# A decoder step whose planner's table of durations is corrected to what its trace shows

## The chip, the cores and the metric

The kernel runs on one core of one Trainium2 chip. TensorE (PE in the rows, with PEld for its weight loads) multiplies, VectorE (DVE), ScalarE (ACT) and GpSimd (POOL) compute, and SyncE (SP) issues most transfers. The metric is the device time of one execution in microseconds, and the time of a kernel is the median of its runs.

## The reference

One step of a hybrid decoder layer in float32, for a prompt of 1024 tokens and for 8 samples of one token each with 1024 cached tokens in pages. Cut to what matters:

```python
h = rms_norm(x, norm_g) * (1.0 + scale[:, None]) + shift[:, None]      # scale, shift, gate = c @ w_ada + b_ada
proj = h @ w_in                     # q, keys and values, gates of attention, z_a, u, v, z_b, g_a, g_b
...
def nsa_core(...):                  # 8 heads of 64, 2 groups of keys
    p_c = softmax(q kc) * mc        # compressed keys: one for each 32 tokens
    imp = p_c.sum(heads), by blocks of 64 keys
    _, idx = lax.top_k(imp, 8)      # the 8 blocks that a query sees
    o_s = softmax(q k_sel) v_sel    # selected blocks
    o_w = softmax(q kw) vw          # window of 512
...
s_b = tril(W_s) @ layer_norm(v) + b            # in chunks of 128 tokens, then u * s_b
out = x + gate * ((sig(g_a) * (silu(z_a) * o) @ w_a + sig(g_b) * (silu(z_b) * u * s_b) @ w_b) @ w_out)
```

It also returns the new key and value rows and the updated window buffers.

## The kernel before, in words

Nearly all products are made in float32r from high and low halves: a product `A B` becomes `Ah Bh + Ah Bl + Al Bh`, three matmuls into one bank of PSUM. The names show it: `hh` and `hl` are the halves of h, `c0h`, `c0l`, `c1h`, `c1l` those of a block of weights of 128 columns (`c0` and `c1` alternate).

The stages follow each other: modulation and h (in the profile the first 75 us), the token-major projections (to 250 us), the attention of the samples (to 430 us), the attention of the prompt (to 790 us), the merge and the output projection.

Beside the two attentions run the channel-major projections, "fills" in what follows: jobs (`stream(jobs)`) that multiply 128 columns of weights by h in pieces of 344 tokens, 24 matmuls to a piece, six at a time: `mm<-hh,c0h`, `mm<-hh,c0l`, `mm<-hl,c0h`, and the same again. There are 2016 of these matmuls. What of them isn't done when the attention of the prompt ends is done behind it. They have the last rank.

The order is made by `Plan`, while the program is built. Every operation goes through `Plan.engine`, whose line 217 is the line of all instructions in the profile. The work is written as streams (Python generators), each of which yields when it would have to wait for a tile or a bank. `Plan.go` picks the next step: the first in rank among the streams whose awaited time has been reached by TensorE's planned clock, or else the one that waits least. The awaited times are kept by `Plan.op`, which adds the duration that `Plan.cost` gives for an operation to the time at which its engine and its operands are free. `Plan` computes nothing of the result, and what comes out of it is only the order of the instructions of each engine; the engines then wait for each other by semaphores. A clock at its lower level is planned too (`cold`).

In the attention of the prompt there are 16 tiles, (group of heads, 128 queries). `front` turns the queries (`R`), multiplies them by the compressed keys (`mx<-kc,R`), makes the probabilities `ce` and from them `pg` (on GpSimd), and takes the maxima of the scores: `maxima` writes four (head, key tile) pairs to a bank of `mx` (`mx<-L,R`, with the masks `mx<-tri_bf,ident_bf` and `mx<-far_bf,ident_bf` added by bf16 matmuls), and DVE reduces the bank to `bm` (selected branch) or `wm` (window). `BT` is made from these and turned. `scores` writes `st<-R,L` (two matmuls), ACT and others make the exponentials `pt` and their halves `p`, and `outputs` multiplies them by the values, `pv<-p,vv`. There are two banks of each of the tags `mx`, `st`, `pv` and `mm`.

In the attention of the samples the pages of keys are gathered (`gk`, by GpSimd, four buffers) and turned, four blocks at a time, in two halves for each sample (`mx<-main,gk` x4, `turn4`); the scores (`st<-kh,qpad`, `st<-kl,qpad`) of a half come one step later. `drop("gk")` after the second half lets the next gather be issued. `red` is the sum by which pages are compressed.

Of the kernel before, what the change touches and what calls it, by code (L numbers as in the profile page):

```python
# [9 lines left out]
F32 = mybir.dt.float32  # L10
FR = mybir.dt.float32r
# [17 lines left out]
class Pack:  # L29
    """Constants that depend on the shapes alone, as columns of one [128, n] array."""  # L30
# [62 lines left out]
class Plan:  # L93
    """Estimates when the engines get to what has been emitted, so that independent streams of work can be
    emitted in an order in which the engines wait little. It has no part in what is computed."""
# [4 lines left out]
    def __init__(self):  # L100
        self.free, self.bus, self.slots, self.rings, self.seen = {}, 0.0, {}, {}, {}
        self.columns, self.streams, self.last = {}, [], 0.0
        self.gone, self.since, self.spilled = 0.0, {}, {}

# [7 lines left out]
    def slot_free(self, uid, name, bufs):  # L112
        """When the next tile of a ring can be written."""
        key = uid, name, self.rings.get((uid, name), 0) % bufs
        return max([x[2] + 60.0 for x in self.seen.get(key, ())] + [0.0])

    def leave(self, uid):
        """The memory of a pool goes to those that come later, when the accesses to it are over."""
# [12 lines left out]
    def meet(x, y):  # L131
        """Whether two accesses to a tile, as box() gives them, overlap."""
# [8 lines left out]
    def after(self, ap, writes_only, engine=None):  # L141
        """When the accesses to the elements of ap are over."""
# [22 lines left out]
    def cost(self, engine, name, outs, ins, size, start):  # L165
        if engine == "pe":
            n, m, dt = ins[1].free_size(), ins[0].free_size(), ins[0].dtype
            cost, passes = max(n / 2.4 + 2.5, (26 if dt == BF else 104) * m / 128), 1
            if name == "transpose":
                passes = 2  # L170
            elif dt == F32:
                cost, passes = max(4 * n / 2.4, 208 * m / 128), 4
            tick = int(start // self.TICK)
            self.columns[tick] = self.columns.get(tick, 0.0) + passes * n * ins[0].partition_size() / 128
            return cost * (2 if self.cold(start) else 1)
        if engine == "dve":
            plain = name == "tensor_copy" and outs[0].space == ins[0].space
            return 67 + (0.52 if plain else 1.042) * size
        if engine == "act":
            return (280 if len(ins) > 1 else 70) + 0.834 * size  # L180
# [51 lines left out]
    def add(self, gen, rank, filler=False):  # L232
        """A stream of work. It yields None to go on when its last step is done, 0 to go on at once, a time or an AP
        to go on when that is reached or written, a function to go on when that is true."""
        self.streams.append([rank, gen, 0.0, None, filler])

    def go(self, until=None, slack=-100.0):
        """Runs the streams, a step of the first in rank that would not wait, until there are none (or until())."""
# [21 lines left out]
def nsa_gmlp_step(ctx: ExitStack, tc: tile.TileContext, a: dict):  # L260
# [29 lines left out]
    def free_bank(tag):  # L290
        """Goes on when a bank can be written, as far as other streams let it."""
# [15 lines left out]
    def rows(name, n, m=128):  # L307
        """The n elements of an input on each of m partitions."""
# [38 lines left out]
    def rsqrt(out, x, scale, n, p=128):  # L347
        """out = (x * scale + EPS) ** -0.5"""
# [24 lines left out]
    def weights(todo):  # L373
        """Loads slices (key, source, columns) in order and cuts them into hi and lo, but for those used as they are."""
# [46 lines left out]
    def x_turned(first):  # L421
        """RMS-normalised x, transposed: every other tile."""
# [26 lines left out]
    def x_loads():  # L449
        """The tiles of x behind the weights of the modulation, which all wait for."""  # L450
# [38 lines left out]
    def modulation():  # L489
        """Shift and scale of the samples and the prompt (column 8), and from them h."""  # L490
# [54 lines left out]
    def h_split():  # L545
        """h as its halves, as it comes."""
# [27 lines left out]
    def rope_tab(which):  # L574
        """[cos * g | sin * g'] so that rope(x * g) = x * cos_g + swap(x) * sin_g"""
# [9 lines left out]
    def constants():  # L585
        """What P1 needs beside its weights, each in time."""
# [25 lines left out]
    def fold(i, p, n):  # L612
        """The rows of the hi and lo halves of the samples, added."""
# [12 lines left out]
    def norm_rope(p, m, i, nh, t, final, done, x=None):  # L626
        """rope(rms_norm(p) * g) into the parts of final: (first head, end, out)"""
# [85 lines left out]
    def gate_rows():  # L713
        """The gate rows of the modulation, to DRAM until the end."""
# [137 lines left out]
    class Chunk:  # L852
        """128 columns of a weight as hi and lo [128, k, 128]."""
# [17 lines left out]
    def paced():  # L871
        """Whether the jobs are not ahead of the attention, so that they last as long as it does."""
# [27 lines left out]
    def stream(jobs):  # L900
        """Jobs of (source of weights, body, condition): the weights of the next job load while this one runs."""
# [24 lines left out]
    def gate_tanh(p, n):  # L926
        """tanh(p / 2), so that p * sigmoid(p) = p * (1 + tanh(p / 2)) / 2"""
# [24 lines left out]
    def z_body(br, c):  # L952
        """silu(z) of a branch, times x where that is there, to DRAM until the merge."""
# [13 lines left out]
    def products(br):  # L967
        """What the projection of a branch takes, as its halves."""
# [23 lines left out]
    def gate_job(br, c):  # L992
        """tanh of half the merge gates of 128 channels, to DRAM until the merge."""
# [14 lines left out]
    def merge_job(br, j):  # L1008
        """Two chunks of 128 channels of a branch in model width, times the gate: all of m, or added to it."""
# [44 lines left out]
    def hand_over():  # L1054
        """When the rotary parts are done, their space goes to the weights of the jobs."""
# [967 lines left out]
```

## Time and profile before

| | us |
|---|---|
| median of 3 runs (lowest, highest) | 1042.51 (1041.81, 1042.57) |
| profiled execution: span from the first to the last instruction | 1039.6 |
| TensorE busy in it | 1018.3 (98%) |
| DVE, ACT, GpSimd busy | 657.1, 468.5, 305.5 |

The profile has no other time of the profiled execution than its span; the median of the runs is 2.9 us above it. A matmul's busy time in the rows outlasts the start of the next one, since matmuls are pipelined, so what a matmul costs is read from the distance of the starts. TensorE's granted clock was 1.00 in the mean, which is its upper level (2.4 GHz).

### The profile page before, as it was taken

To read this page: it belongs to the slowest core of one execution; us is meant where nothing else is said; L and a number is where in the kernel's file an instruction comes from. 1 tells how busy PE (TensorE), PEld (TensorE's weight loads), DVE (VectorE), ACT (ScalarE), POOL (GpSimd) and SP (SyncE) were. 2 spreads that over 40 slices of the span, in tenths; PEclk is the share of its full clock that TensorE was granted. 3 is DMA by queue.
4 is the path that set the end of the run, shared out by engine and by line. 5 is a ranking of instruction groups with operands and counts; after the bars stand their busy time and mean duration, and the time that the engine had idled before them with its cause. 6 is when DMAs were issued, how large, how long until landed. Compare 5 with 4: busy or idle time off the path is not lost. (4 is left out here: it accounts for less than half of the span.)

```text
span 1039.6 us, 16376 instructions
## 1 busy us (share of the span) xinstructions
PE 1018.3 (98%) x5747; PEld 878.7 (85%) x5747; DVE 657.1 (63%) x1372; ACT 468.5 (45%) x984; POOL 305.5 (29%) x332
## 2 busy tenths in 40 slices
PE   7999999999999999999999999999999999999998
PEld 2589977879999999987878788778788999998776
DVE  5676786354668766578787868895753147675322
ACT  5763332001332244767766677677666242232000
POOL 0453565454221110013334332433333100251000
PEclk9999999999999999999999999999999999999999
DMA  9735451103875745521212121211111478554321
GB/s 328 263 95 175 135 185 52 61 22 129 277 213 149 256 152 192 151 67 41 79 53 72 35 64 49 68 38 51 50 58 59 126 248 254 187 163 146 120 91 62
DMA packets 106311, 130.33 MB, mean 125 GB/s; under 512 B 27299, under 2 KB 71525, under 8 KB 106230
## 3 DMA queue, kind: packets, MB, share of 16 engines
q1 hardware_dynamic: 101622, 112.52, 33.7%
q0 software_dynamic: 4608, 16.78, 5.2%
q8 instruction: 45, 0.74, 0.3%
q14 instruction: 36, 0.29, 0.1%
HBM read 98.95 MB, written 30.23 MB: 124 GB/s over the span
## 5 line engine op out<-in xcount | busy, mean ns | idle before, releaser
L217 PE MATMUL pv<-p,vv 128*128 128x512 f32 (+1 forms) x396 | 111.7, 399 | 0.5 <-DVE p L217 0.4
L217 PE MATMUL mm<-hh,c0h 128*128 128x344 f32 x320 | 105.3, 329 | 0.0
L217 ACT ACTIVATE pt<-st 128x512 f32<-128x512 f32 x132 | 78.7, 596 | 58.5 <-PE st L217 56.1
L217 PE MATMUL mm<-hh,c1h 128*128 128x344 f32 x320 | 104.9, 328 | 0.0
L217 PE MATMUL mm<-hl,c0h 128*128 128x344 f32 x320 | 102.3, 320 | 0.0
L217 PE MATMUL mm<-hl,c1h 128*128 128x344 f32 x320 | 102.2, 319 | 0.0
L217 PE MATMUL mm<-hh,c1l 128*128 128x344 f32 x320 | 102.2, 319 | 0.0
L217 PE MATMUL mm<-hh,c0l 128*128 128x344 f32 x320 | 102.2, 319 | 0.0
L217 PE MATMUL st<-R,L 128*128 128x512 f32 (+1 forms) x264 | 88.2, 415 | 0.0
L217 PEld LDWEIGHTS pv<-p,vv 128*128 128x128 f32 (+1 forms) x396 | 65.7, 172 | 22.4 <-DVE p L217 1.9
L217 DVE TENSOR_TENSOR p<-pt,p 128x512 fp32r<-128x512 f32 x88 | 69.4, 794 | 17.7 <-ACT p L217 17.1
L217 POOL TENSOR_TENSOR p<-pt,p 128x512 fp32r<-128x512 f32 x44 | 60.0, 1364 | 53.9 <-ACT p L217 53.9
L217 ACT ACTIVATE p<-pt 128x512 fp32r<-128x512 f32 x94 | 59.1, 629 | 13.6 <-POOL pt L217 12.3
L217 POOL TENSOR_SCALAR_AFFINE_SELECT pt<-pt 128x512 f32<-128x512 f32 x40 | 29.3, 732 | 121.7 <-ACT pt L217 119.8
L217 PE MATMUL mx<-L,R 128*128 128x512 f32 (+3 forms) x204 | 61.7, 364 | 1.8 <-DVE bm L217 1.1
L217 PEld LDWEIGHTS mm<-hh,c1h 128*128 128x128 f32 x320 | 60.3, 188 | 2.9 <-issue 0.2
L217 PEld LDWEIGHTS mm<-hh,c0h 128*128 128x128 f32 x320 | 60.4, 189 | 2.5 <-issue 0.2
L217 PEld LDWEIGHTS mm<-hh,c1l 128*128 128x128 f32 x320 | 60.3, 188 | 2.5
L217 PEld LDWEIGHTS mm<-hh,c0l 128*128 128x128 f32 x320 | 60.3, 188 | 2.1
L217 PEld LDWEIGHTS mm<-hl,c0h 128*128 128x128 f32 x320 | 60.1, 188 | 0.0
L217 PEld LDWEIGHTS mm<-hl,c1h 128*128 128x128 f32 x320 | 60.1, 188 | 0.0
L217 ACT ACTIVATE th<-mm 128x344 f32<-128x344 f32 x68 | 30.9, 454 | 58.3 <-PE mm L217 58.0
(497 smaller groups left out, 2669.3 us busy)
## 6 DMA issues: line engine op xcount, KB each, us to landing
t_db<-th SPq DMA_DIRECT2D x24, 172.0 KB
t_da<-th SPq DMA_DIRECT2D x24, 172.0 KB
th<-t_db SPq DMA_DIRECT2D x24, 172.0 KB
th<-t_da SPq DMA_DIRECT2D x24, 172.0 KB
graw<-in_w_ada_dram SPq DMA_DIRECT2D x16, 256.0 KB
araw<-in_w_ada_dram SPq DMA_DIRECT2D x16, 256.0 KB
xt<-in_x_dram SPq DMA_DIRECT2D x8, 512.0 KB
eraw<-in_w_ada_dram SPq DMA_DIRECT2D x16, 256.0 KB
```

Source lines behind the costliest of these rows:

```text
L217: r = getattr(real, name)(*args, **kw)
```

## The change

The durations in `Plan.cost` are replaced, and an attribute is added that holds the form of TensorE's last instruction. Nothing else differs but comments. No operation is added, removed or given to another engine.

```diff
 def __init__(self):
+        self.form = "split"
...
     def cost(self, engine, name, outs, ins, size, start):
         if engine == "pe":
             n, m, dt = ins[1].free_size(), ins[0].free_size(), ins[0].dtype
-            cost, passes = max(n / 2.4 + 2.5, (26 if dt == BF else 104) * m / 128), 1
-            if name == "transpose":
-                passes = 2
-            elif dt == F32:
-                cost, passes = max(4 * n / 2.4, 208 * m / 128), 4
+            form, passes, turn = "split", 1, 0.0
+            if dt == FR and name != "transpose":
+                cost = max(0.4375 * n + 7, 104 * m / 128)
+                turn = {"split": 0.0, "full": 85.0, "part": 190.0}[self.form]
+            elif name == "transpose" or dt == BF:
+                form, passes = "full", 2 if name == "transpose" else 1
+                cost = max(0.4375 * n + 7, (26 if dt == BF else 104) * m / 128)
+                turn = 190.0 if self.form == "part" else 0.0
+            elif m <= 64 and n > 128:
+                form, passes, cost = "part", 4, 0.4375 * n * 4 * m / 128 + 3
+                turn = 0.0 if self.form == "part" else 140.0
+            else:
+                form, passes, cost = "full", 4, max(4 * (0.4375 * n + 7), 208 * m / 128)
+                turn = 190.0 if self.form == "part" else 0.0
+            self.form = form
             tick = int(start // self.TICK)
             self.columns[tick] = self.columns.get(tick, 0.0) + passes * n * ins[0].partition_size() / 128
-            return cost * (2 if self.cold(start) else 1)
+            return cost * (2 if self.cold(start) else 1) + turn
         if engine == "dve":
             plain = name == "tensor_copy" and outs[0].space == ins[0].space
+            if name == "reciprocal":
+                return 80 + 18 * size
             return 67 + (0.52 if plain else 1.042) * size
         if engine == "act":
-            return (280 if len(ins) > 1 else 70) + 0.834 * size
+            moved = ins and self.box(ins[0])[1][0] != self.box(outs[0])[1][0]
+            return (280 if len(ins) > 1 else 70) + 0.834 * size + (105 if moved else 0)
```

Here `n` is the number of columns that a matmul streams, `m` the columns of its weights, `FR` float32r, `BF` bf16 and `F32` plain float32. `moved` is an activation whose output begins on another partition than its input.

The new order differs in most of the two attentions. The first place is TensorE's order in the seventh tile of the prompt's attention, behind the second bank of maxima; `L_4485` and `L_4363` are the same keys, `R` the queries, `far_bf` and `tri_bf` the masks. Before:

```order
L217 MATMUL mx<-L_4485,R 128x384
L217 LDWEIGHTS ident_bf
L217 MATMUL mx<-far_bf,ident_bf 128x128
L217 MATMUL st<-R,L_4484 128x512
L217 MATMUL st<-R_5516,L_4487 128x512
L217 MATMUL mm<-hh,c0h 128x344
L217 MATMUL mm<-hh,c0l 128x344
L217 MATMUL mm<-hl,c0h 128x344
L217 MATMUL mm<-hh,c0h 128x344
L217 MATMUL mm<-hh,c0l 128x344
L217 MATMUL mm<-hl,c0h 128x344
L217 MATMUL mx<-L_4485,R 128x256
```

And after:

```order
L231 MATMUL mx<-L_4363,R 128x384
L231 LDWEIGHTS ident_bf
L231 MATMUL mx<-far_bf,ident_bf 128x128
L231 MATMUL st<-R,L_4362 128x512
L231 MATMUL st<-R_5313,L_4365 128x512
L231 MATMUL mx<-L_4363,R 128x256
L231 LDWEIGHTS ident_bf
L231 MATMUL mx<-tri_bf,ident_bf 128x128
L231 MATMUL mx<-L_4363,R 128x256
L231 LDWEIGHTS ident_bf
L231 MATMUL mx<-far_bf,ident_bf 128x128
L231 MATMUL mx<-L_4363,R 128x384
```

The six fills between the scores and the next maxima are gone from here.

The second place is TensorE's order in the keys of the samples, from one half's turned keys to the next half's; `main` holds the identity, `qpad` the queries of the samples. Before, up to the second of them (ahead of these rows stand the first, its two score matmuls and one more fill):

```order
L217 MATMUL mm<-hh,c0l 128x344
L217 MATMUL mm<-hl,c0h 128x344
L217 MATMUL mm<-hh,c0h 128x344
L217 MATMUL mm<-hh,c0l 128x344
L217 MATMUL mm<-hl,c0h 128x344
L217 MATMUL mm<-hh,c0h 128x344
L217 MATMUL mm<-hh,c0l 128x344
L217 MATMUL mm<-hl,c0h 128x344
L217 MATMUL mm<-hh,c0h 128x344
L217 MATMUL mm<-hh,c0l 128x344
L217 MATMUL mm<-hl,c0h 128x344
L217 MATMUL mx<-main,gk 128x128 x4
```

And after, with both:

```order
L231 MATMUL mx<-main,gk 128x128 x4
L231 MATMUL pv<-pd,red 128x32
L231 MATMUL st<-kh,qpad 128x512
L231 MATMUL st<-kl,qpad 128x512
L231 MATMUL mm<-hh,c1h 128x344
L231 MATMUL mm<-hh,c1l 128x344
L231 MATMUL mm<-hl,c1h 128x344
L231 MATMUL mm<-hh,c1h 128x344
L231 MATMUL mm<-hh,c1l 128x344
L231 MATMUL mm<-hl,c1h 128x344
L231 MATMUL mx<-main,gk 128x128 x4
```

Of the 12 fills between the two halves six are left; in the other half of a sample there are 12 as before.

## Rows read from the trace of the kernel before

**Rows 1.** The page's first line.

```profile
span 1039.6 us, 16376 instructions
```

**Rows 2.** Busy time (instructions) of PE, PEld, DVE, ACT, POOL by stretch; clock, DMA share, GB/s.

```profile
0.00:75.00 75.00, 66.93 (x314) 40.35 (x315) 49.95 (x127) 49.68 (x108) 25.63 (x45) 1.00 0.68 236
75.00:250.00 175.00, 174.40 (x890) 148.61 (x889) 108.61 (x235) 40.99 (x81) 90.09 (x78) 1.00 0.31 99
250.00:430.00 180.00, 177.88 (x1178) 172.18 (x1179) 119.36 (x217) 69.18 (x158) 33.39 (x37) 1.00 0.65 207
430.00:790.00 360.00, 354.44 (x2032) 296.43 (x2031) 267.98 (x599) 249.93 (x537) 121.77 (x137) 1.00 0.19 57
790.00:1035.00 245.00, 244.69 (x1342) 221.11 (x1340) 109.92 (x195) 58.69 (x104) 34.61 (x36) 1.00 0.48 152
```

**Rows 3.** Timeline of PE, keys of the samples: start us, duration us, [idle before <-releaser].

```profile
259.10 0.63 PE L217 MATMUL mx<-main,gk 128*128 128x128 f32 x4 [1.27 <-DVE red L217]
...
268.19 0.60 PE L217 MATMUL mx<-main,gk 128*128 128x128 f32 x4
...
274.00 0.60 PE L217 MATMUL mx<-main,gk 128*128 128x128 f32 x4
...
275.12 0.32 PE L217 MATMUL mm<-hh,c0h 128*128 128x344 f32 x1
...
276.85 0.32 PE L217 MATMUL mm<-hl,c0h 128*128 128x344 f32 x1
277.59 0.63 PE L217 MATMUL mx<-main,gk 128*128 128x128 f32 x4 [0.41 <-DMA gk<-in_cache_k_slc_dram,idx]
```

**Rows 4.** Timeline of PE, the seventh tile of the prompt's attention.

```profile
534.87 0.53 PE L217 MATMUL mx<-kc,R 128*128 128x64 f32 x4
...
536.99 0.23 PE L217 MATMUL mx<-far_bf,ident_bf 128*128 128x128 bf16 x1
...
538.94 0.42 PE L217 MATMUL mx<-L,R 128*128 128x384 f32 x1
...
539.43 0.40 PE L217 MATMUL mm<-hh,c0h 128*128 128x344 f32 x1
539.67 0.32 PE L217 MATMUL mm<-hh,c0l 128*128 128x344 f32 x1
```

**Rows 5.** DVE's groups by form, 430 to 790 us: busy us, mean ns | idle before.

```profile
L217 DVE TENSOR_TENSOR p<-pt,p 128x512 fp32r<-128x512 f32 x84 | 66.6, 798 | 12.7 <-ACT p L217 12.2
L217 DVE TENSOR_REDUCE bm<-mx 128x8 f32<-128x512 f32 x72 | 47.5, 682 | 4.1 <-PE mx L217 3.8
```

**Rows 6.** Timeline of DVE at the place of rows 4.

```profile
536.61 1.34 DVE L217 TENSOR_REDUCE wm<-mx 128x4 f32<-128x512 f32 x2
```

**Rows 7.** Waits of PE, 430 to 790 us: us in total, times, longest.

```profile
PE mx L217 <- DVE bm L217: 1.7, 4, 0.8
PE mx L217 <- DVE BT L217: 1.6, 2, 1.0
PE mx L217 <- DVE s L217: 0.6, 1, 0.6
...
PE mx L217 <- DVE wm L217: 0.2, 1, 0.2
```

**Rows 8.** Timelines of PE and POOL: the chain to `pg` in two tiles.

```profile
540.25 0.41 POOL L217 TENSOR_TENSOR pg<-ce,gates 128x128 f32<-128x128 f32 x1
...
702.81 0.53 PE L217 MATMUL mx<-kc,R 128*128 128x64 f32 x4
...
707.01 0.40 POOL L217 TENSOR_TENSOR pg<-ce,gates 128x128 f32<-128x128 f32 x1 [2.92 <-DVE ce L217]
```

**Rows 9.** The gathers `gk` on POOL, 250 to 300 us.

```profile
DMA to landing us min/median/max: 4.2/5.1/8.4
```

**Rows 10.** Timeline of PE in the modulation.

```profile
16.84 1.02 PE L217 MATMUL mm<-araw,cT 128*9 128x512 f32 x2
```

**Rows 11.** ACT's groups by form, 430 to 790 us.

```profile
L217 ACT ACTIVATE R<-mx 32x128 fp32r<-32x128 f32 x64 | 17.1, 267 | 7.2 <-PE mx L217 6.4
```

## The prediction

> **What bounds the kernel now.** I read the page first, then the stages, then the waits of each stage, then the timeline around the places where the order of TensorE's instructions changes. The span is 1039.6 us [rows 1], and in the five stretches [rows 2] TensorE's busy times add up to 1018.3. They show where the rest lies: length minus busy is 8.1 us in the first 75 us, 0.6 us in the token-major projections, 2.1 us in the decode attention, 5.6 us in the prompt attention, and 0.3 us in the end. The granted clock is 1.00 throughout, so no stretch gains or loses by it. A program of fixed TensorE work that is 98% busy gets faster only by shorter waits (about 17 us of them, 8 in the beginning, which the change hardly reorders), and slower by longer ones. In the attention the other engines are near: DVE works 268 and ACT 250 of 360 us. The fills (2016 matmuls of 344 columns) cover them.
>
> **Is the corrected number right?** Twelve fills in a row start from 275.12 to 276.85, 0.157 us each [rows 3]; the old table says 344/2.4+2.5 = 146 ns, the new one 157.5. Behind a masking matmul of the form "full" the step is 539.43 to 539.67, 0.24 us [rows 4], so 0.08 more: the new turn of 85 ns. DVE's reductions of a maximum (682 ns) and its products of probabilities (798 ns) [rows 5] stand at 67+1.042x512 = 600 ns in both tables. So before, TensorE's fills were planned 7% short and DVE's long operations 12% and more, and the plan was nearly a true picture on a faster clock. Now TensorE alone is right, and what it waits for is still planned short. That is the core of my forecast: a fill is now thought to cover 7% more than before, so fewer are put into a chain, while the chain is as long as it was.
>
> The Trainium skill, TensorE: Matmul & The Clock Gate, section Back-to-back issue gap, gives N/2.4+2.5 ns for an isolated matmul at the upper clock, which is the old table and speaks against the change. The trace does not agree: 157 ns instead of 146. By the rule the fills that I count below as withdrawn would be worth 26 us instead of 28, and the sum would be smaller by half a microsecond.
>
> **The change part by part.** No work is added. TensorE's order has 292 turns from full to split instead of 298; at the 0.08 us above that is **-0.5 us**.
>
> Prompt attention. By the order, 708 fills stand in it instead of 888, and 540 behind it instead of 258 (102 fewer stand ahead of it). 180 x 0.157 = 28 us of cover leave a stage whose waits are 5.6 us. What is late next is the pair of `mx` banks: the maxima write one, DVE reduces it (`bm`, `wm`), and two writes later TensorE needs it again. The first place in the order above is such a one: the bank closed at 536.99 is written again at 538.94, 1.95 us later, with DVE's two reductions over at 536.61+1.34 = 537.95 [rows 4, 6]. Without the six fills the second write comes 0.94 us sooner, at 538.0, so here it just fits. I did this for all 111 places where a write follows a `bm` or `wm` reader, adding the start-to-start times of what stands between. Two queued reductions take 1.3 us [rows 6]; cover under that is had at 7 places before and 27 after, and what is missing adds up to 2.6 and 9.0 us: **+6.4 us**. The check: the trace's waits of matmuls for `bm` and `wm` are 1.7 and 0.2 us in five places [rows 7], and as a matmul's row (0.32 us) outlasts its step (0.16), each such wait is longer than it shows by 0.16, so 2.7 us, against 2.6 counted. Bounds: with an answer of 1.0 us (DVE with a short queue; one reduction and the way there and back) it is 0.9 to 2.2, +1.3; with 1.5 us (a further product ahead in DVE's queue) 4.6 to 15.3, +10.7. I take the middle one because it is the one that meets the trace.
>
> The other chain of a tile goes from the scores of the compressed keys (`mx<-kc,R`) to the gated probabilities (`pg`), which TensorE then turns. It takes 534.87 to 540.66, 5.8 us, in the seventh tile, and 702.81 to 707.41, 4.6 us, in the fourteenth [rows 4, 8]. By the order TensorE's cover is 6.1 us or more in all 16 tiles before; after, it is 3.99 in the fourteenth, 4.73 to 5.73 in six others. With 4.6 us everywhere 0.6 us are missing, with 5.8 us 4.3. I take **+0.6 us**, the value of the tile that is shortest.
>
> Decode. Before, 12 fills stand between the turned keys of one half of a sample and those of the next; after, 6 and 12 in turn (second place above). Each load has four buffers and its gather is issued when an earlier one is dropped. From the second half of one sample to the first of the sample after next is 268.19 to 277.59 us before; without the 0.41 us waited for the gather, and the 0.16 us that the row hides, 8.83 us [rows 3]. After it is 12 fills less, 8.83-12x0.157 = 6.95 us. Gathers land 4.2/5.1/8.4 us after issue [rows 9]: the median stays covered, the slowest is late by 8.4-6.95 = **+1.5 us**. The first keys already wait 1.27 us for `red` [rows 3], and come six fills (0.9 us) sooner, with nothing to bring the gather forward: **+0.9 us**. Bounds for decode: 0 (the slow one was issued early) and +6 (four late ones).
>
> The first 75 us and the token-major projections. The order there is almost the one before. The new table gives `mm<-araw,cT` 66+140 ns, but two of them take 1.02 us [rows 10], so they are still planned short, and I see no place in the order that this moves against a wait. 0, within 1.5 us either way.
>
> ACT's 105 ns and DVE's reciprocals. `R<-mx` over 32 partitions takes 267 ns [rows 11]; the old table said 70+0.834x128 = 177, the new 282. This is the one part that makes the plan of other engines truer, and it acts the right way (more cover ahead of `BT` and `R`). Its effect is already in the order I counted.
>
> Sum: -0.5+6.4+0.6+1.5+0.9 = **+8.9 us**. The profiled execution's span of 1039.6 us becomes 1048.5; the runs' median, 1042.51, lies 2.9 us above it, which I carry over: **1051 us**.
>
> **The rivals.** *Same* (within 0.2%, some 2.1 us, which is what a measurement of this kernel can tell): the withdrawn fills were surplus, as at the first place, where the bank is free at 537.95 and would be asked for at 538.0; and the answer to a lone reduction is 1.0 us. Then -0.5+1.3+0.9 = +1.7, 1044 at most. Against it: DVE's load rises from 74 to some 81% of a stage shorter by 28 us, so that two reductions queue oftener.
> *Faster*: the moved evictions, now planned 105 ns longer each (four `R` in a row, 0.42 us), put cover where TensorE waits for `BT` (1.6 us, two times) and `s` (0.6 us) [rows 7] and for what ACT gives. If these 2.2 us go, the 0.5 us of turns, and about half of the 1.9 us at the banks, it is -3.7, **1039**. It decides in favour of this if DVE answers a bank within 0.95 us, the cover at the first place; the shown queue of two is against it.
> *Decode bound by its gathers*: the period of a sample falls from 5.81 us (268.19 to 274.00) [rows 3] to 4.87 (six fills less); if landings, not TensorE, set the pace then, each of the six later samples loses the 0.94 again, 5.6 us in place of the 1.5: +13 in all, **1055**.
>
> **How the numbers follow.** My forecast, +4 to +12 us, gets 0.54; decode bound, above, 0.12; same, 0.15; faster by over 2.1 us, 0.19. Together slower 0.66, same 0.15, faster 0.19. The likeliest case alone gives 1046 to 1055; eight in ten take in part of the faster case (down to 1039) and the upper bound of the banks with some of decode's (up to 1062).
>
> **What would show it.** Right: the attention shorter by about 20 us, the end longer by some 44 (282 x 0.157), TensorE's waits for `bm` and `wm` two to four times the 1.9 us, in about 20 places; the decode with one or two waits for `gk` above 1 us. Wrong: waits for `bm` and `wm` as now although the fills are gone (DVE had idle time just there), or the waits for `BT` and `s` gone; or a new wait in the first 75 us, where I claim nothing moves.

## The result, and the profile after

The changed kernel takes 1081.58 us (median of 4 runs) against 1042.44 us before: a ratio of 1.038, 95% interval 1.0365 to 1.0395. The direction was forecast, the size was not: +39 us instead of +9, far outside the range.

First the span and the stretches, as in [rows 1] and [rows 2], but with the border at 802 us, where the last output of the prompt's attention starts.

```profile
span 1079.7 us, 16393 instructions
```

```profile
0.00:75.00 75.00, 62.20 (x259) 34.36 (x260) 46.42 (x114) 45.77 (x96) 26.95 (x41) 0.95 0.69 227
75.00:250.00 175.00, 174.21 (x875) 146.82 (x874) 106.83 (x243) 42.49 (x88) 88.26 (x80) 1.00 0.32 100
250.00:430.00 180.00, 173.15 (x1146) 165.79 (x1144) 121.08 (x219) 68.30 (x155) 35.52 (x40) 1.00 0.62 197
430.00:802.00 372.00, 350.94 (x1933) 281.23 (x1933) 267.33 (x601) 253.30 (x544) 126.51 (x142) 1.00 0.18 53
802.00:1075.00 273.00, 273.00 (x1541) 251.96 (x1539) 111.62 (x195) 58.66 (x105) 29.52 (x30) 1.00 0.48 148
```

In the kernel before, that border lies at 805 us and not at the 790 of [rows 2]. Its row there:

```profile
430.00:805.00 375.00, 369.44 (x2112) 309.60 (x2111) 272.31 (x606) 259.54 (x555) 126.71 (x142) 1.00 0.19 58
```

TensorE's idle time grows in three places: 12.8 us in the first 75 (8.1 before), 6.9 in the samples' attention (2.1), 21.1 in the prompt's (5.6). In the first stretch the granted clock, 1.00 before, is 0.95 in the mean.

Idle time misses the part of a wait that a matmul's row hides. So below I count a wait as what the distance of two starts exceeds the usual one of the same shapes, behind and ahead of the same forms, in the kernel before. By this count TensorE's work is 1001.7 us in both traces, and its waits are 27.4 us before and 67.2 after: 39.8 us, the whole difference of the spans (40.1). Steps that are longer because the clock was lower are in it. By stages, the first up to the last turned tile of x, then up to the first turned keys `gk`, to the first `mx<-kc,R`, to the last `pv<-p,vv`, to the end:

| waits, us | first | projections | samples | prompt | end |
|---|---|---|---|---|---|
| before | 8.3 | 3.5 | 2.8 | 12.0 | 1.0 |
| after | 17.6 | 5.0 | 7.7 | 36.7 | 0.2 |

What is called usual is a choice: with the median or the lower quartile of each distance single entries move by up to 4 us, the differences between the two kernels by about 1.

TensorE's waits in the attention of the prompt, 430 to 802 us (total, times, longest), answer to [rows 7]:

```profile
PE mx L231 <- DVE BT L231: 4.3, 5, 1.5
PE mx L231 <- DVE bm L231: 3.2, 5, 0.8
PE mx L231 <- DVE s L231: 2.8, 5, 1.4
PE pv L231 <- POOL p L231: 2.8, 4, 1.2
PE mx L231 <- DVE wm L231: 2.6, 8, 0.5
PE mx L231 <- DVE ce L231: 2.4, 3, 1.4
PE mx L231 <- ACT pgT L231: 1.5, 3, 0.7
```

The banks behind `bm` and `wm`, on which the prediction put nearly all, are 5.8 of these 19.6 us. Five other answers are late too, and longer than before.

The place of [rows 4] and [rows 6] in the kernel after, first TensorE's rows and then DVE's:

```profile
533.51 0.23 PE L231 MATMUL mx<-far_bf,ident_bf 128*128 128x128 bf16 x1
533.54 0.71 PE L231 MATMUL st<-R,L 128*128 128x512 f32 x2
...
534.52 0.44 PE L231 MATMUL mx<-L,R 128*128 128x384 f32 x1
```

```profile
533.13 1.33 DVE L231 TENSOR_REDUCE wm<-mx 128x4 f32<-128x512 f32 x2
```

The reductions end at 534.46 and the bank is written at 534.52: the six fills were surplus here, as computed. It is otherwise where DVE has other work. At a later tile the bank is wanted behind six fills and two score matmuls, and DVE is in the selection and the output of another tile:

```profile
637.73 0.63 PE L231 MATMUL st<-R,L 128*128 128x512 f32 x2
639.20 0.30 PE L231 MATMUL mx<-main,pg 128*128 128x128 f32 x1 [0.84 <-DVE bm L231]
```

```profile
637.42 0.72 DVE L231 TENSOR_SCALAR imp<-imp 128x16 f32<-128x16 f32 x1
638.06 0.19 DVE L231 RECIPROCAL s<-s 128x8 f32<-128x8 f32 x1
638.28 0.17 DVE L231 TENSOR_TENSOR s<-s,g 128x8 f32<-128x8 f32 x1
638.37 1.28 DVE L231 TENSOR_REDUCE bm<-mx 128x8 f32<-128x512 f32 x2
```

The reductions begin only when three operations of other chains are over, at 638.37; the answer is not two reductions but whatever stands ahead of them in DVE's order. (The first of the three takes 0.72 us and not some 0.17; the last section comes back to it.) And a whole chain can be late, here that of `BT`, behind six fills of which the last starts at 502.66. TensorE's row, then two of DVE's ahead of it:

```profile
504.47 0.30 PE L231 MATMUL mx<-main,BT 128*128 128x128 f32 x1 [1.49 <-DVE BT L231]
```

```profile
503.01 0.51 DVE L231 TENSOR_SCALAR BT<-cst 128x4 f32<-128x4 f32 x1
503.62 0.70 DVE L231 TENSOR_SCALAR BT<-cst 128x8 f32<-128x8 f32 x1
```

In the samples' attention the two waits that were forecast are there (TensorE's timeline, then the gathers, as in [rows 3] and [rows 9]):

```profile
267.51 0.63 PE L231 MATMUL mx<-main,gk 128*128 128x128 f32 x4 [2.30 <-DVE red L231]
...
283.82 0.63 PE L231 MATMUL mx<-main,gk 128*128 128x128 f32 x4 [2.00 <-DMA gk<-in_cache_k_slc_dram,idx]
```

```profile
DMA to landing us min/median/max: 4.5/5.9/8.1
```

### The profile page after: what moved, and what is told of

Its sections match the earlier page's. It is cut to its first block, busy times and chain, and to the rows that moved or that the text cites. A ratio compares the mean times of both kernels' runs of the same rounds, so it can differ in the third digit from the quotient of the medians.

```text
span 1079.7 us, 16393 instructions
## 1 busy us (share of the span) xinstructions
PE 1033.5 (96%) x5747; PEld 880.2 (82%) x5747; DVE 654.7 (61%) x1372; ACT 468.5 (43%) x984; POOL 306.8 (28%) x332
## 5 line engine op out<-in xcount | busy, mean ns | idle before, releaser
L231 PE MATMUL mm<-hh,c1h 128*128 128x344 f32 x280 | 91.7, 327 | 0.0
L231 PE MATMUL mm<-hh,c0h 128*128 128x344 f32 x280 | 91.1, 326 | 0.0
L231 PE MATMUL mm<-hh,c0l 128*128 128x344 f32 x280 | 89.5, 320 | 0.6 <-DVE c0l L231 0.6
L231 PE MATMUL mm<-hl,c0h 128*128 128x344 f32 x280 | 89.4, 319 | 0.0
L231 PE MATMUL mm<-hh,c1l 128*128 128x344 f32 x280 | 89.4, 319 | 0.0
L231 PE MATMUL mm<-hl,c1h 128*128 128x344 f32 x280 | 89.4, 319 | 0.0
L231 ACT ACTIVATE p<-pt 128x512 fp32r<-128x512 f32 x94 | 59.1, 629 | 21.2 <-POOL pt L231 16.7
L231 POOL TENSOR_TENSOR m<-m,th 128x344 f32<-128x344 f32 x24 | 25.2, 1070 | 143.1 <-DVE th L231 143.1
L231 PEld LDWEIGHTS mm<-hh,c0l 128*128 128x128 f32 x280 | 52.7, 188 | 3.2 <-DVE c0l L231 0.9
L231 PEld LDWEIGHTS mm<-hh,c0h 128*128 128x128 f32 x280 | 52.7, 188 | 2.9 <-issue 0.4
L231 PEld LDWEIGHTS mm<-hh,c1l 128*128 128x128 f32 x280 | 52.7, 188 | 1.9
```

Of the source, the lines that this page charges most:

```text
L231: r = getattr(real, name)(*args, **kw)
```

## The experiments

The fills are counted here from the first to the last row of the prompt's maxima and outputs, as in the expectations (846 before, 654 after). Theory A is that of the prediction in its general form: TensorE's durations grew and the others' did not, so the plan puts too little cover into the chains. All but e15, e16 and e17 ran once; the kernel before, which ran beside them, lay between 1039.55 and 1042.68 us, so that 3 us between single runs say nothing. "Waits" are those of the table above.

**One half of the change each.** e1 takes back ACT's and DVE's entries, e2 has only them.

```diff
# e1, against the change
-            if name == "reciprocal":
-                return 80 + 18 * size
-            moved = ins and self.box(ins[0])[1][0] != self.box(outs[0])[1][0]
-            return (280 if len(ins) > 1 else 70) + 0.834 * size + (105 if moved else 0)
+            return (280 if len(ins) > 1 else 70) + 0.834 * size
# e2: these lines of the change, in the kernel before
```

> The new durations of TensorE alone; ACT's 105 ns and DVE's reciprocals are taken back. Theory A (TensorE's cover is now planned longer than what it covers, because TensorE's durations grew and those of DVE, ACT and GpSimd stayed about a tenth short): the whole loss is there, 1078 to 1086 us; by the order 606 fills stand in the attention of the prompt (654 with the whole change, 846 before, counted from the first maxima to the last output), so if anything a little slower than 1081.6. Rival B (the lengthened moved activations and reciprocals put the order of the prompt's attention out of step): most of the loss goes, under 1060 us. Rival C (any change of the table costs about as much, since the order before was a lucky one): 1060 to 1100, no relation to the count of fills.

> The table of before with only ACT's 105 ns for moved operands and DVE's reciprocals corrected. Theory A: TensorE's scale is unchanged, 834 fills in the attention (846 before), so 1038 to 1048 us. Rival B: 1060 us or more. Rival C: any, likely 1055 or more, though the count of fills is that of before.

e1: 1090.42 us, waits of the prompt's attention 41.2 us. e2: 1050.74, waits there 19.2. So the loss is TensorE's table (e1 lies above theory A's range, on its side). ACT's and DVE's entries cost 9.6 us alone, though the whole change is 9 us faster with them than without. That e2 should stay under 1048 was wrong.

**The scale.** e3 shortens TensorE's new durations, e4 lengthens the others', e8 lengthens TensorE's old ones.

```diff
# e3, against the change
-            return cost * (2 if self.cold(start) else 1) + turn
+            return 0.93 * (cost * (2 if self.cold(start) else 1) + turn)
# e4, against the change
-            cost = self.cost(engine, name, outs, ins, size, start)
+            cost = self.cost(engine, name, outs, ins, size, start) * (1 if engine == "pe" else 1.1)
# e8, against the kernel before
-            return cost * (2 if self.cold(start) else 1)
+            return 1.07 * cost * (2 if self.cold(start) else 1)
```

> The whole change, with all of TensorE's new durations (turns too) times 0.93, so that the scale of TensorE to the other engines is about that of before, while the corrected proportions among TensorE's own forms stay. Theory A: most of the loss goes; 780 fills in the attention, a third of the way from before to the change, so 1045 to 1060 us. Rival D (it is the proportions: turns and the part form put the first 75 us and the chains wrong): stays above 1070. Rival C: any, likely 1055 or more.

> The whole change, and the durations of DVE, ACT and GpSimd times 1.1, to about what the trace shows. Theory A: the scales fit again and the fills come back into the attention (858 by the order; 846 before), so 1038 to 1055 us. Rival D: stays above 1070. Rival C: 1055 or more.

> The table of before with all of TensorE's durations times 1.07 and nothing else: the scale of the change with the proportions of before. 738 fills in the attention (846 before, 654 with the change). Theory A: a good part of the change's loss, 1052 to 1068 us, by waits in the prompt's attention, the first stage as before. Rival D (turns and forms, not the scale): 1040 to 1047.

e3: 1062.21 us (waits in the prompt's attention 19.6); e4: 1059.04 (15.7); e8: 1056.82 (19.1). Half or more of the loss goes with the scale from either side, and the new scale of TensorE alone makes 15 us (e8). But e3 and e4 lie 2 and 4 us above theory A's ranges, and e4 has 858 fills in the attention, more than the kernel before, with more waits (15.7 instead of 12.0). In e3 and e4 the first stage keeps its loss (16.2 and 14.0 us of waits), so it has another cause.

**The turns.** e10 is the change without them, e11 the kernel before with one of them.

```diff
# e10, against the change
-            return cost * (2 if self.cold(start) else 1) + turn
+            return cost * (2 if self.cold(start) else 1)
# e11, against the kernel before
+            split = dt == FR and name != "transpose"
+            turn, self.form = 85.0 if split and not self.form else 0.0, split
...
-            return cost * (2 if self.cold(start) else 1)
+            return cost * (2 if self.cold(start) else 1) + turn
```

> The whole change with the turns (85, 140 and 190 ns) at nothing. The slopes of the new table stay. 798 fills in the attention (654 with the turns, 846 before). Theory G (the turns, which the old table did not have at all, take more cover than the 7% of the slope): the attention's waits fall to 18 to 24 us, 1060 to 1070 us. Rival (the slope is what counts): 1075 or more.

> The table of before with one thing of the new one: 85 ns when a split matmul follows another form. 732 fills in the attention (846 before; 738 when all of TensorE's durations were planned 1.07 times as long, which gave 1056.8). Theory G: 1054 to 1066 us, waits of the attention 18 to 26 us. Rival: 1042 to 1049.

e10: 1069.86 us; the waits of the prompt's attention are 19.5, and those of the first stage even 22.2. e11: 1062.03, waits of the attention 24.5. So the turn of 85 ns alone adds more waits to that stage (12.5 us) than a slope of 7% does (7.1 in e8). Both leave nearly the same number of fills in it (732 and 738), so the difference isn't one of their count.

**The cover itself.** e9 leaves every duration of the change and asks for a margin.

```diff
# e9, against the change
-    plan.go(until=lambda: 1 in closed)
+    plan.go(until=lambda: 1 in closed, slack=400.0)
```

> The whole change, but in the attention of the prompt a stream counts as ready only when TensorE's planned clock is 400 ns past its awaited time (before and in the change: 100 ns ahead of it). The durations stay those of the change; only the cover grows: 1026 fills in that attention by the order (654 with the change). Theory A (the loss of that stage is lost cover, whatever the table says): the stage's waits fall from 36.7 us to 8 to 16, 1055 to 1064 us; what is left is the first stage and the decode, which the edit leaves alone. Rival F (the new order itself is the trouble, such as which stream comes first at an engine): still above 1072.

e9: 1063.61 us. The waits in the attention fall from 36.7 to 10.5, less than before the change, with 1026 fills there (846 before): with enough cover that stage's loss goes, whatever the durations say. Its rows answer to the first list above:

```profile
PE mx L231 <- DVE BT L231: 2.0, 4, 0.8
PE mx L231 <- DVE wm L231: 1.7, 5, 0.5
PE mx L231 <- DVE bm L231: 0.3, 1, 0.3
```

But 162 fills are left behind it, and the end waits 8.3 us (1.0 before). e12 shows that side more strongly, with too much cover in the kernel before.

```diff
# e12, against the kernel before
-            cost = self.cost(engine, name, outs, ins, size, start)
+            cost = self.cost(engine, name, outs, ins, size, start) * (1 if engine == "pe" else 1.1)
```

> The table of before with the durations of DVE, ACT and GpSimd times 1.1, about as the trace has them; TensorE's stay short. It gives more cover than before: 888 fills in the attention and 144 behind it (258 before), at the banks 0.7 us missing at an answer of 1.3 us (2.6 before). Theory A: the attention's 12 us of waits fall to 6 to 10, so 1035 to 1043 us, unless the first stage gets out of step (then up to 1050). Rival C: 1050 or more.

e12: 1070.72 us, a miss of 28. The end, with 144 fills, waits 17.1 us, and the attention 16.7 (12.0 before), although 888 fills stand in it. In this stretch behind the attention TensorE is busy for 85 of 100 us and its clock falls:

```profile
800.00:900.00 100.00, 85.28 (x456) 76.14 (x455) 38.45 (x75) 43.05 (x88) 18.85 (x23) 0.90 0.45 137
```

The fills are a budget: what is added in the attention is missing in the merge, where 162 fills (e9) and 144 (e12) were too few.

**The first stage.** e5 takes the form `part` out of the change, e6 puts it alone into the kernel before.

```diff
# e5, against the change
-            elif m <= 64 and n > 128:
-                form, passes, cost = "part", 4, 0.4375 * n * 4 * m / 128 + 3
-                turn = 0.0 if self.form == "part" else 140.0
# e6, against the kernel before
+            elif dt == F32 and m <= 64 and n > 128:
+                cost, passes = 0.4375 * n * 4 * m / 128 + 143, 4
```

> The whole change without the form part: the matmuls of the modulation with 9 columns of weights and 512 streamed are again planned at about 0.9 us instead of 0.07 (0.21 with its turn). Behind the first 75 us or so the order on TensorE is that of the change. Theory E (the wrong price of this form is what costs the first stage its 6 to 9 us): 1072 to 1077 us, with waits of the first stage near the 8.3 us of before. Rival (the first stage is lost by the new scale of TensorE, as the attention is): 1080 to 1083.

> The table of before with only this form at its new price (69 ns and a turn of 140). Behind the first stage the order on TensorE is that of before. Theory E: 1047 to 1052 us, the loss all in the first stage. Rival: 1040 to 1044.

e6: 1049.92 us, the waits of the first stage 15.8 instead of 8.3: this price alone costs what the theory said. e5: 1082.63, and 15.5 us there: taking it out gives nothing back in the time, against the theory, and 2.1 us in that stage's waits. In both runs a part is the clock. Here are the first 75 us of e5:

```profile
0.00:75.00 75.00, 63.42 (x272) 38.21 (x273) 47.21 (x114) 46.54 (x99) 23.44 (x41) 0.93 0.69 229
```

The mean clock of that stretch is 0.93 in e5, 0.95 in e6 and in the kernel after, and 1.00 before. The missing shares of 75 us, 5 and 4 us, are an estimate of what the clock can have taken there; over the whole span e5's clock was 0.991 in the mean and that of the kernel after 0.996, which is 5 us more. So e6 shows that the price of this form is enough to put the stage out of step; what it costs inside the whole change e5 doesn't settle. In e5, in e6 and in the kernel after, the last product with the modulation's weights (`araw`) comes late, at 40.13 us in e5, at 40.52 in e6. Here it is in the kernel before, and then in the kernel after:

```profile
36.54 1.02 PE L217 MATMUL mm<-graw,cT 128*9 128x512 f32 x2
37.40 1.02 PE L217 MATMUL mm<-araw,cT 128*9 128x512 f32 x2
```

```profile
41.29 1.02 PE L231 MATMUL mm<-graw,cT 128*9 128x512 f32 x2
42.15 1.02 PE L231 MATMUL mm<-araw,cT 128*9 128x512 f32 x2
```

One of them costs 0.86 us by the starts (36.54 to 37.40; a row with x2 is one product, which the trace has as two records); the old table said 4x512/2.4 = 853 ns, the new one 66 and a turn of 140. Here the correction replaced a true number by a false one.

**One stage each.** e13 has the new table until h is there, e14 in the prompt's attention alone. In both the old formulas stand beside the new ones, and a flag chooses.

```diff
# e13 and e14, in cost(), against the change
+            if not self.new:
+                ...
+                return cost * (2 if self.cold(start) else 1)
# e13 starts with self.new = True
     plan.go(until=lambda: len(h_ready) == NT + 1, slack=100.0)
+    plan.new = False
# e14 starts with self.new = False
     plan.go(until=lambda: "decode" in over and jobs_done[0] >= b_jobs)
+    plan.new = True
```

> The new table for the first stage alone (until h is there), the old one from then on. Behind the first stage the order on TensorE is that of before. If the stages' losses add up (theory H), this is the first stage's 6 to 9 us: 1048 to 1052 us, and waits in the attention of the prompt as before, 11 to 13 us. Rival: the first stage's loss is made good later, 1041 to 1044.

> The new table for the attention of the prompt alone, the old one until then. 678 fills in it (654 with the whole change, 846 before). Theory H: this stage's loss alone, waits of 30 to 38 us there instead of 12: 1060 to 1068 us. Rival: the attention lost because of what it was handed by the stages before it, under 1055.

e13: 1048.67 us (before, in the same runs, 1041.59), waits of the first stage 16.6. e14: 1062.98, waits of the attention 34.5. The two lose 7.1 and 21.4 us, 28.5 of the 39; of the rest 6.4 us are the waits that the projections and the samples' attention gained.

**How much any disturbance costs, and a version that beats both.** e7 makes a step that corrects nothing; e16 gives the kernel before a little more margin; e15 and e17 give the new table its margin in the attention alone, e17 without ACT's and DVE's entries; e18 is one of these entries alone.

```diff
# e7, against the kernel before
-            cost, passes = max(n / 2.4 + 2.5, (26 if dt == BF else 104) * m / 128), 1
+            cost, passes = max(n / 2.4 + 3.0, (26 if dt == BF else 104) * m / 128), 1
# e15 and e17, against e14; e16 (with 0.0), against the kernel before
-    plan.go(until=lambda: 1 in closed)
+    plan.go(until=lambda: 1 in closed, slack=150.0)
# e17 also, as e1; e18, against the kernel before: the two lines on `moved` of the change
```

> The table of before with 3.0 instead of 2.5 ns behind n/2.4: TensorE's durations 0.3% longer, which corrects nothing. It asks how much any disturbance of the order costs. Theory A (scale): 1042 to 1048 us, since 804 fills stand in the attention instead of 846 and the banks are covered better than before (1.2 us missing at an answer of 1.3 us, 2.6 before). Rival C (the order before was a lucky one): 1050 us or more.

> The kernel before, with a margin of 0 instead of 100 ns ahead in the attention of the prompt: 882 fills in it and 222 behind it. It asks whether the kernel before had the right amount of cover. Theory A: 1036 to 1043 us, waits of the attention 7 to 12 us. Rival C: 1046 or more.

> As the one before, and in that stage a stream counts as ready only when TensorE's planned clock is 150 ns past its awaited time, instead of 100 ns ahead of it. 870 fills in the attention and 240 behind it (846 and 258 before). Theory A: with the cover back, and the true proportions, the waits are 8 to 13 us, 1036 to 1044 us, a candidate to beat the kernel before. Rival (the corrected proportions themselves are bad for the order): 1048 or more.

> As e15 (new table and a margin of 150 ns in the attention of the prompt alone), but without the 105 ns of ACT and the reciprocals: only TensorE's corrected durations are left of the change. 870 fills in the attention and 240 behind it, the same as in e15. Theory I (with equal cover the rest of e15's 18.5 us of waits comes from the corrected ACT and DVE entries, as in e2): waits there 10 to 14 us, 1039 to 1045 us. Rival J (it comes from TensorE's corrected proportions, or from the draw of the order): waits of 16 us or more, 1046 or more.

> The table of before with only ACT's 105 ns for moved operands. 852 fills in the attention (846 before, 834 in e2). Theory I, by this entry: waits in the attention of 17 to 21 us as in e2, 1047 to 1052 us. Rival: 11 to 14 us, 1041 to 1045, and e2's loss is that of the reciprocals, or of the two together.

| | us | against before | fills in the attention, behind | waits of the attention |
|---|---|---|---|---|
| e7 | 1043.93 | one run | 804, 306 | 12.0 |
| e16 | 1042.66 | 1.0004 to 1.0024 | 882, 222 | 12.8 |
| e15 | 1049.45 | 1.0051 to 1.0084 | 870, 240 | 18.5 |
| e17 | 1050.94 | 1.0070 to 1.0104 | 870, 240 | 19.9 |
| e18 | 1044.71 | one run | 852, 252 | 12.8 |

e7 costs next to nothing, so not every disturbance does. e15 missed its range (1036 to 1044 us). Against e14 its margin takes the waits from 34.5 to 18.5 us, with 870 fills instead of 678. But e15 and e17 have nearly as many fills in the attention as e16 and 6 to 7 us more of waits: the count alone doesn't make the time. That where the fills stand makes the rest is likely, but not shown. That ACT's and DVE's entries were the reason (as e2 suggested) fell with e17, which has none of them. And e18 loses 3 us where e2 lost 9.6, against its theory, so e2's loss is that of the reciprocals or of the two together. TensorE's waits in the attention in e17:

```profile
PE mx L237 <- DVE BT L237: 3.4, 4, 1.2
PE mx L237 <- DVE s L237: 1.6, 4, 0.8
PE mx L237 <- DVE bm L237: 1.4, 4, 0.6
PE mx L237 <- DVE wm L237: 1.0, 3, 0.5
```

The chain to `BT` leads it. No version beats the kernel before; e16 comes nearest, 0.04 to 0.24% above it.

## Why the prediction was wrong

**The mechanism was right, its price was not.** Fills withdrawn from the attention (180 by the prediction's count) leave TensorE waiting for other engines: e9 gives more cover with the durations unchanged and the waits go, e15 gives back slightly more than the old number of fills and 16.0 of e14's 22.5 us of added waits go; e3, e4 and e8 show the scale working in both directions. The stage lost 24.7 us where +7.0 was forecast. Of the signs, the waits for `bm` and `wm` came (three times the 1.9 us, in 13 places), so did the longer end (273 us instead of 230) and one gather late by 2 us; the attention, 3 us shorter instead of 20, did not, and the new wait in the first 75 us, a sign of being wrong, did.

**The reason given for it was wrong.** The prediction held that the old table had DVE's long operations 12% short, as rows of 682 and 798 ns stand against 600 planned, so that the old plan was "nearly a true picture on a faster clock". It took DVE's cost from the length of a row, and that of the fills from the distance of the starts. By their starts DVE's operations of 512 columns follow each other at 0.60 us, which is the old table's price:

```profile
516.06 0.68 DVE L231 TENSOR_REDUCE wm<-mx 128x4 f32<-128x512 f32 x1
516.66 0.68 DVE L231 TENSOR_TENSOR p<-pt,p 128x512 fp32r<-128x512 f32 x1
517.26 0.68 DVE L231 TENSOR_REDUCE wm<-mx 128x4 f32<-128x512 f32 x1
```

(They are of the kernel after; the price is the same in both tables.) ACT's exponentials (`pt<-st`) follow at 0.49 us, planned at 0.50. So of these long operations only TensorE's were planned short, and the factor of 1.1 in e4 and e12 made DVE's and ACT's longer than they are. The likely account is that a TensorE planned too short worked as a margin, since an answer planned true then asks for more fills; the correction took that margin away, and what the plan doesn't know (the last section has one such delay) became waits. That e9 and e15 gain by a margin fits this; no run tests it against the draw of the order. The direction didn't hang on the wrong reason, since the fills were counted in the order itself.

**The term that failed: the attention, priced at two reductions per bank.** The banks behind `bm` and `wm` gained some 5 us of waits (3.8 to 8.5), for which +6.4 stood. What was left out: banks whose last reader is another, above all `ce` on DVE and `pgT` on ACT (+4.9, none before); `BT` itself (2.0 to 5.1); `s` (1.1 to 2.8); the probabilities `p`, now those of GpSimd (0.8 to 4.3); and delays without idle time in the rows (3.5 to 8.3). Most of these chains were covered before, so [rows 7] showed little or nothing of them; for `BT` and `s`, which it did show, no growth was priced. The chain to `pg`, forecast at +0.6, made no wait for its own data.

**The step that a fill "is now thought to cover 7% more".** It named the slope and put the turns down only as a gain of 0.5 us. By e11 the turn alone makes 12.5 us of waits in that stage. It must move TensorE's planned clock past the answers as the slope does, and more so where masks and turned tiles stand between the fills; that is argued. This step is not in the sum, since the fills were counted in the new order, turns included.

**The first stage, "0, within 1.5 us either way", was wrong by 9.3 us of waits.** The step was that the order "is almost the one before": in the trace it changes from TensorE's nineteenth record on. The row of 1.02 us [rows 10] was read as two products, and is one. So the old table had planned them right (853 ns for 0.86 us), and the new one made them short by 0.65, which the prediction took for no matter. With the form's price alone the loss is there (e6); without it, too, as far as e5 can tell. Which of the other entries does it is open: the turn alone makes 3.5 us (e11), the slope in the old proportions 1.9 (e8), and the change without turns 13.9 (e10, whose clock in the first 75 us was 0.91). Part of it is the lower clock, by the estimate above up to 4 us.

**The samples' attention.** The two terms came nearly as forecast: the first keys wait 1.0 us longer (2.30 instead of 1.27 shown; +0.9 forecast) and one gather is late by 2.00 instead of 0.41 (+1.5 forecast). Further waits for `red` and `tm` (1.7 us) and smaller ones made 4.9 of the forecast 2.4. The gathers did not set the pace: only this one was waited for.

**The gap between matmuls.** The trace's 157 ns [rows 3] are not in doubt, and the table with 146 ns made the faster order. The Trainium skill, TensorE: Matmul & The Clock Gate, section Back-to-back issue gap, gives N/2.4 + 2.5 ns for an isolated matmul, from which these 146 ns are an estimate; the trace doesn't agree. A price in this plan works by its ratio to the others.

**Open.** With nearly equal fills the corrected table has 6 to 7 us more of waits (e15, e17), and is 7 to 8 us slower than e16. Whether that is its proportions or the draw of one order among many isn't settled; e7 and e16 are two draws near the old order, not a sample of them.

## What to carry to other kernels

A table that only orders work is a set of ratios, and an error in it can be what keeps the order good: here TensorE's durations were 7% short, and making them true cost 3.8%. Lengthening the other engines (e4) or adding a margin (e9, e15) gave about half of the loss back or more, but no corrected table reached the old order, so measure a correction before you keep it. Read all durations in the same way, by the distance of the starts. Count what covers the chains as a budget, since the stage behind needs its share. And when cover goes, price every chain that it covered by what stands ahead of it in its engine's order; here those with little or no wait in the trace before (`ce`, `pgT`, `p`, `s`) gained more than the two that were priced.

## What was not expected of the hardware

A DVE operation on four elements in each partition can take 1.04 us. Here are DVE's row and GpSimd's, in the kernel after:

```profile
647.94 1.04 DVE L231 TENSOR_SCALAR BT<-cst 128x4 f32<-128x4 f32 x1
```

```profile
647.62 1.33 POOL L231 TENSOR_TENSOR p<-pt,p 128x512 fp32r<-128x512 f32 x1 [0.34 <-ACT p L231]
```

They end together (648.98 and 648.95), and over all 24 operations `BT<-cst` (of 4 to 32 elements) the minimum, median and maximum are 171/220/1065 ns (170/172/423 before). It is no single case. The late reductions above stood behind a selection step (`imp`) of 0.72 us, from 637.42 to 638.14, and GpSimd was in this operation until 638.11:

```profile
636.82 1.29 POOL L231 TENSOR_TENSOR p<-pt,p 128x512 fp32r<-128x512 f32 x1
```

Of the 32 operations of DVE on `BT<-cst` and `imp<-imp` in the prompt's attention, 13 take more than 0.4 us after the change and 5 before, most others some 0.17; each of these 18 ends 26 to 37 ns behind the end of a GpSimd operation that had begun before it. The Trainium skill, SBUF — State Buffer, section SBUF: two separate sides, says that some DVE operations and those of GpSimd lock a shared pair of ports for a whole instruction; the trace agrees in these rows, but no run here tries it alone. In the first tile shown here TensorE then waits 1.27 us for `BT`, and in the one at 504.47 above the two rows of DVE are longer by 0.9 us together than the usual 0.17 each. `Plan` has no such delay, so some of the answers that it counts on get late by what stands on GpSimd at that moment.

The clock: in the first stage of the kernel after the granted clock is 0.96 and 0.90 in the second and third 25 us, and 1.00 before. It is near its lower level (1.2 GHz) from 48 to 55 us. In the 4 us ahead of that TensorE was busy for 2.5 us, as it waited for `hx` on ACT and for halves of weights (`bh`, `bl`).

```profile
25.00:50.00 25.00, 21.90 (x83) 7.98 (x81) 16.69 (x36) 15.71 (x31) 9.21 (x12) 0.96 0.72 227
50.00:75.00 25.00, 23.98 (x133) 22.08 (x134) 19.46 (x57) 18.87 (x46) 16.04 (x24) 0.90 0.47 157
44.00:48.00 4.00, 2.47 (x13) 1.47 (x11) 3.40 (x10) 3.98 (x10) 0.88 (x2) 0.99 0.40 104
48.00:55.00 7.00, 6.68 (x22) 5.74 (x22) 4.38 (x10) 4.61 (x11) 3.88 (x5) 0.52 0.58 201
```
